# A hybrid diffusion backbone on one core: the low parts of U by VectorE, a transposed selection layout, and a gather whose last steps are spread

## The chip, the cores and the metric
One core of a Trainium2 chip runs the whole program in one launch. The metric is device time in microseconds (us) of that core; the median of several executions counts. Engines: PE is TensorE, DVE is VectorE, ACT is ScalarE, POOL is GpSimd, SP is SyncE, which issues most of the DMAs.

## The reference, cut to what matters
Two layers over 256 latent and 256 context tokens of width 1024. A layer is a token mixer followed by PEER, an expert retrieval, and the change touches PEER only (and in its second layer only the selection):

```python
q = (x @ wq).reshape(t, 8, 2, 64)
s = einsum('thpd,hpnd->thpn', q, keys)          # 2 x 128 scores per token and head
sv, si = lax.top_k(s, 16)
cand = sv[:, :, 0, :, None] + sv[:, :, 1, None, :]
best, pos = lax.top_k(cand, 16)                 # 8 heads x 16 experts per token
g = softmax(best)
act = gelu(einsum('tkd,td->tk', u_tab[eidx], x))
out = einsum('tk,tkd->td', g * act, v_tab[eidx])
```

There are 16384 experts of width 1024. The first layer handles all 512 tokens, the second one only the 256 latent tokens. Everything is float32.

## The kernel before
The kernel does not gather the experts of most tokens. It multiplies all of U with all tokens, weights the result with a mostly-zero gate matrix, and multiplies that with all of V. A float32 product is made of three matmuls over a high part `h` (rounded by ACT) and a low part `lo` (what rounding left, a subtraction on DVE or POOL); `halves` (L1221) makes both parts of a tile.

**Tiles of U and V.** U and V of a layer come in 128 tiles of 128x1024, 512 KB each. `u_mm` (L1235) is the product of tile j of U with the tokens: 24 matmuls into a PSUM tile `po`, of which there are two, po0 and po1, used in turn; ACT's Gelu empties it into `ga`. `split_u` (L1225) makes the parts `wh` and `wl` of U one tile ahead. Which engine makes `wl` is read from `lo_eng[0]`, and if that is None, POOL makes the odd tiles of the first layer and DVE the rest. During the routing `lo_eng[0]` is DVE in the first layer; at its end it is set to None, so POOL works in the sweep.

**The sweep** (the loop over j in the section that begins with `with ExitStack() as dx`): per tile of V, `gate` multiplies `ga` with the gate tile G and splits it into `Wh` and `Wl`, `split_v` makes `vh` and `vl` one tile ahead, and `v_mm` adds 18 matmuls of 512 columns per tile to six accumulators (three groups of 128 tokens in the first layer). Products of U run ahead of V by up to 20 tiles at the start and 10 from tile 64 on, so a tile of V and a product of U alternate on PE until tile 118, and after that V is alone.

**The gather.** In the first layer, the first 128 context tokens are not swept. `gather` (L1288) fetches their experts' rows with 256 indirect DMAs issued by POOL into three buffers `grow`, first 128 of U (a dot product on DVE, L1299), then 128 of V (a weighted sum on DVE into `gacc`, L1303). At its end it transposes `gacc` on PE in two halves into a `po` tile each (L386 is the transpose) and adds them to the stream `hT` (L1315). The sweep takes two steps of the generator per tile from tile 2, and a third on odd tiles from 25. Its 256 steps before the last part are used up at tile 109, where both halves of the last part are also made.

**The rows of the next layer's modulation** (`mod_rows`, 40 units in the first layer) start only when the generator of the gather is exhausted: two rows per tile from then on, the rest after the loop. Each row is a 512 KB load into the same `grow` buffers and two dot products on DVE for the first 16 rows (L512), one for the other 24 (L520). What DVE does in these steps is issued behind `vl` of the next tile (`issue_after(late.ins)`). After the loop, the sums of V are copied by ACT into `grow` buffers too (L1759), transposed, and added to `hT` (L1767); then the second layer begins.

**The selection** (`select`, L1400) runs once per group of 128 tokens, four times in the first layer and twice in the second, on DVE: 16 best of 60 candidates for each of 8 heads (`top16`), then arithmetic over 128 numbers per token on the positions. `best` and `pos` lie heads-outermost (8x16), `ab2` lies heads-innermost (16x8), so several instructions write with a stride. `scatter` builds the gate matrix from it. In the first layer the last selection, of the gathered tokens, comes after the last scatter; `fill` holds the early products of U, and one step of it is made per step of the routing.

**The order of the work.** The instructions of an engine are put in order by a planner at build time: what is ready sooner goes first, and among ready ones what the program emits first; a buffer is given to its next user when the last reader of the old content is done. On the chip every queue then runs in that order. So SP's loads, POOL's gathers and DVE's work each wait behind what stands ahead of them.

Of the kernel before, what the change touches and what calls it, by code (L numbers as in the profile page):

```python
# [8 lines left out]
F32 = mybir.dt.float32  # L9
F32R = mybir.dt.float32r  # L10
F16 = mybir.dt.float16
U32 = mybir.dt.uint32
I32 = mybir.dt.int32
AF = mybir.ActivationFunctionType
ALU = mybir.AluOpType
AX = mybir.AxisListType
# [3 lines left out]
P = 128  # L20
# [245 lines left out]
def body(ctx, tc, I, out, dbg=None):  # L266
# [21 lines left out]
    def po_tile():  # L288
        tick[0] ^= 1
        return psp.tile([P, 512], F32, name=f"po{tick[0]}")  # L290
# [62 lines left out]
    fill = Filler()  # L353
# [31 lines left out]
    def transpose(o, i):  # L385
        pe.transpose(o, i, ident)  # L386
# [183 lines left out]
    for l in range(DEPTH):  # L570
        last = l == DEPTH - 1
# [649 lines left out]
        def halves(h, lo, r, eng=dve):  # L1221
            act.activation(h, r, AF.Copy)  # L1222
            return eng.tensor_tensor(lo, r, h.bitcast(F32), op=ALU.subtract)  # L1223

        def split_u(j):  # L1225
            if j >= P:
                return
            h = wp.tile([P, D], F32R, name="wh", bufs=3)
            lo = wp.tile([P, D], F32R, name="wl", bufs=3)
            halves(h, lo, ur.pop(j), lo_eng[0] or (pool if not last and j % 2 else dve))  # L1230
            us[j] = (h, lo)

        def u_mm(j):
# [32 lines left out]
        def early(upto):  # L1266
            while nu[0] < upto:
                u_next()
                yield
# [12 lines left out]
        def gather():  # L1282

            rows = lambda: up.tile([P, D], F32, name="grow", bufs=3)
            gix, gw = gsel
            dot = up.tile([P, P], F32, name="gdot")
            for p, tab in ((0, I['UR']), (1, I['V'][l].rearrange("j i d -> (j i) d"))):
                q = []  # L1288
                for e in range(P + 2):
                    if e < P:  # L1290
                        q.append(rows())
                        pool.indirect_dma_start(out=q[-1], out_offset=None, in_=tab,  # L1292
                                                in_offset=bass.IndirectOffsetOnAxis(ap=gix[:, p, e:e + 1], axis=0))
                    if e < 2:
                        continue
                    e -= 2
                    g = q.pop(0)
                    if p == 0:
                        dve.scalar_tensor_tensor(g, g, 1.0, mtok, op0=ALU.mult, op1=ALU.mult, accum_out=dot[:, e:e + 1])  # L1299
                    elif e == 0:  # L1300
                        dve.tensor_scalar(acc, g, dot[:, e:e + 1], None, op0=ALU.mult)
                    else:
                        dve.scalar_tensor_tensor(acc, g, dot[:, e:e + 1], acc, op0=ALU.mult, op1=ALU.add)  # L1303
                    yield
                if p == 0:
                    act.activation(dot, dot, AF.Gelu)
                    dve.tensor_tensor(dot, dot, gw, op=ALU.mult)
            assert hT_back
            for h in range(2):
                ps = po_tile()  # L1310
                for k in range(4):
                    transpose(ps[:, k * 128:(k + 1) * 128], acc[:, (4 * h + k) * 128:(4 * h + k + 1) * 128])
                for k in range(4):
                    c = 4 * h + k
                    dve.scalar_tensor_tensor(hT[:, c, :128], ps[:, k * 128:(k + 1) * 128], mod[:, 40 + c, 0:1],  # L1315
                                             hT[:, c, :128], op0=ALU.mult, op1=ALU.add)
                yield
# [8 lines left out]
        with ExitStack() as tx:  # L1326
# [14 lines left out]
            KEYS = tk.tile([P, 1024], F32, name="keys")  # L1341
            pool.dma_start(KEYS, I['keys'][l])
            rep = sel.tile([P, 128], F32, name="rep", bufs=1)
            bits = sel.tile([P, 16], U32, name="bits", bufs=1)
            dve.memset(bits, 15)

            def top16(v, ix, x):
# [52 lines left out]
            def select(i):  # L1400

                sv, si = ranked.pop(i)

                lst = sel.tile([P, 2, 16, 8], F16, name="lst")
                act.activation(lst, si.rearrange("p (a h) r -> p a r h", a=2), AF.Copy)
                cand = sel.tile([P, 8, NC], F32, name="cand", bufs=1)
                for a, na, w, o in ROWS:
                    dve.tensor_tensor(cand[:, :, o:o + na * w].rearrange("p h (a b) -> p h a b", a=na),
                                      sv[:, 0:8, a:a + na][:, :, :, None].to_broadcast([P, 8, na, w]),
                                      sv[:, 8:16, :w][:, :, None, :].to_broadcast([P, 8, na, w]), op=ALU.add)  # L1410
                best = sel.tile([P, 8, 16], F32, name="best")
                pos = sel.tile([P, 8, 16], U32, name="pos")
                for h in range(8):
                    top16(best[:, h], pos[:, h], cand[:, h])
                    if h % 2:
                        yield


                ab2 = sel.tile([P, 2, 16, 8], F16, name="ab2")
                A, B = [ab2[:, z].rearrange("p k h -> p h k") for z in range(2)]  # L1420
                sl = sel.tile([P, 2, 8, 16], U32, name="sl", bufs=1)
                dve.tensor_scalar(sl[:, 0], pos, 3, None, op0=ALU.logical_shift_right)
                dve.tensor_scalar(sl[:, 1], pos, 2, None, op0=ALU.logical_shift_right)
                dve.tensor_scalar(A, sl[:, 0], -1.0, 0.0, op0=ALU.add, op1=ALU.max)
                dve.scalar_tensor_tensor(A, sl[:, 1], -5.0, A, op0=ALU.add, op1=ALU.max)
                dve.scalar_tensor_tensor(A, pos, -44.0, A, op0=ALU.add, op1=ALU.max)
                dve.tensor_scalar(sl[:, 0], pos, 16.0, None, op0=ALU.is_ge)
                for c in (32.0, 52.0, 52.0):
                    dve.scalar_tensor_tensor(sl[:, 0], pos, c, sl[:, 0], op0=ALU.is_ge, op1=ALU.add)
                dve.tensor_tensor(sl[:, 1], bits[:, None, :].to_broadcast([P, 8, 16]), sl[:, 0], op=ALU.logical_shift_right)  # L1430
                dve.tensor_tensor(sl[:, 1], pos, sl[:, 1], op=ALU.bitwise_and)
                dve.tensor_copy(B, sl[:, 1])
                ij = ijg[i] = sel.tile([P, 3, 16, 8], F32, name="ij")
                bm = sel.tile([P, 8], F32, name="bm")
                dve.tensor_copy(bm, best[:, :, 0])
                dve.tensor_tensor(best, best, bm[:, :, None].to_broadcast([P, 8, 16]), op=ALU.subtract)

                with tc.issue_after(evac[0].ins) if i < NG else nullcontext():
                    act.activation(best, best, AF.Exp)


                for z in range(2):
                    m = sel.tile([P, 16, 16, 8], F16, name="match", bufs=1)
                    dve.tensor_tensor(m, iotar[:, None].to_broadcast([P, 16, 16, 8]),
                                      ab2[:, z][:, :, None, :].to_broadcast([P, 16, 16, 8]), op=ALU.is_equal)
                    dve.tensor_tensor(m, m, lst[:, z][:, None].to_broadcast([P, 16, 16, 8]), op=ALU.mult)
                    for w in (8, 4, 2):
                        dve.tensor_tensor(m[:, :, :w], m[:, :, :w], m[:, :, w:2 * w], op=ALU.add)
                    dve.tensor_tensor(ij[:, z], m[:, :, 0], m[:, :, 1], op=ALU.add)
                    if z == 0:  # L1450
                        yield
                dve.tensor_reduce(bm, best, axis=AX.X, op=ALU.add)
                dve.reciprocal(bm, bm)
                dve.tensor_tensor(ij[:, 2].rearrange("p k h -> p h k"), best, bm[:, :, None].to_broadcast([P, 8, 16]), op=ALU.mult)
                if i < NG:

                    f = lambda x: x.rearrange("p k h -> p (k h)")
                    gix, gw = gsel
                    dve.scalar_tensor_tensor(gix[:, 0], f(ij[:, 0]), float(P), f(ij[:, 1]), op0=ALU.mult, op1=ALU.add)
                    dve.scalar_tensor_tensor(gix[:, 1], f(ij[:, 1]), float(P), f(ij[:, 0]), op0=ALU.mult, op1=ALU.add)  # L1460
                    dve.tensor_copy(gw, f(ij[:, 2]))
                yield
# [102 lines left out]
            def routing():  # L1565
# [31 lines left out]
                for z, _ in enumerate(end):  # L1597
                    next(others, 0)
                    if z == 8:
                        fill.add(early(ne))  # L1600
                    yield
                if NG:
                    yield from select(0)

# [1 line left out]
                for _ in range(per_step[0]):  # L1606
                    fill.step()
            fill.flush()
            lo_eng[0] = None


        with ExitStack() as dx:
# [205 lines left out]
```

## Time and profile before

| | |
|---|---|
| median of 3 runs | 3116.19 us (3100.6 to 3119.41) |
| the profiled execution | 3115.79 us, its span 3114.0 us |
| PE busy | 2956.3 us (95%) |
| DVE busy | 2339.7 us (75%) |
| ACT busy | 1448.6 us (47%) |
| POOL busy | 664.6 us (21%) |
| DMA | 661.43 MB, mean 212 GB/s |

The span begins with the first layer's mixer (to about 640 us), goes on with its scatter and selections (to 885), its sweep (885 to 1920), the second layer's mixer and routing (to about 2500) and its sweep. A row of busy times by stretch shows for each stretch how long every engine was busy; where PE is not busy all of it, the stretch has a limit other than PE. The granted clock of PE is 1.00 where it ran at 2.4 GHz throughout; a lower number mixes in time at 1.2 GHz. Matmuls of a row overlap: a matmul that lasts 389 ns is issued every 0.23 us.

### The profile page before, as it was taken

The page shows a single profiled execution, that of the slowest core. Times are in us where ns is not written, and L with a number is a line of the kernel's source. Part 1 is how long each engine was busy: PE and PEld are TensorE (multiplying, and loading weights), DVE is VectorE, ACT ScalarE, POOL GpSimd, SP SyncE. Part 2 cuts the span into 40 slices and gives each one's busy share as a digit, 9 for nine tenths or more (in the row PEclk, how much of TensorE's full clock was granted, in tenths as well). Part 3 has the DMA queues.
Part 4 walks back from the last instruction along what each step waited for, and adds up shares of the span by engine and source line. Part 5 has one row for each costly group of instructions (what it writes and reads, how often), then busy time and mean ns, then how long its engine had stood idle before and what let it go on. Part 6 is the DMA issues. An engine that isn't in the chain of part 4 may idle for free.

```text
span 3114.0 us, 47475 instructions
## 1 busy us (share of the span) xinstructions
PE 2956.3 (95%) x17500; PEld 2607.5 (84%) x17500; DVE 2339.7 (75%) x4764; ACT 1448.6 (47%) x2583; POOL 664.6 (21%) x428
## 2 busy tenths in 40 slices
PE   8999999988899999999999998999989999999998
PEld 5877777888788998888888886789988998889986
DVE  5775876799987877877877898868689767555555
ACT  5444422558843333323333234466458654554544
POOL 1001100310044455555555510100060000000000
PEclk9999999999999999999999998999999999999999
DMA  7232345534489888888888876344644689766644
GB/s 267 72 103 87 121 133 173 160 121 156 182 291 309 302 292 308 306 314 289 291 275 294 301 260 236 107 122 126 192 156 170 221 285 306 242 209 209 206 152 151
DMA packets 262504, 661.43 MB, mean 212 GB/s; under 512 B 21464, under 2 KB 113632, under 8 KB 261760
## 3 DMA queue, kind: packets, MB, share of 16 engines
q1 hardware_dynamic: 221808, 513.35, 50.3%
q0 software_dynamic: 40464, 145.05, 13.4%
q8 instruction: 137, 2.24, 0.3%
q14 instruction: 95, 0.78, 0.1%
HBM read 609.03 MB, written 49.29 MB: 211 GB/s over the span
## 4 chain that ended last, share of the span: by engine, by line
PE 49%; DVE 12%; DMA 11%; issue 9%; POOL 6%; ACT 2%; POOLq 0%; DVEq 0%; SPq 0%; ACTq 0%
PE mm L1664 7%; PE at L1664 7%; DMA grow<-in_V_dram,gix 6%; PE po L392 5%; PE po L390 5%; PE po L391 5%; PE mm L390 4%; PE mm L391 4%; PE mm L392 4%; POOL grow L1292 4%; PE at L1526 3%; DMA vr<-in_V_dram 2%; POOL wl L1223 2%; DMA grow<-in_UR_dram,gix 1%; DVE wl L1223 1%
## 5 line engine op out<-in xcount | busy, mean ns | idle before, releaser
L392 PE MATMUL po<-nh,wl 128*128 128x384 f32 (+1 forms) x2048 | 642.4, 314 | 33.8 <-DVE wl L1223 30.4
L390 PE MATMUL po<-nh,wh 128*128 128x384 f32 (+1 forms) x2048 | 642.6, 314 | 13.0 <-DVE hT L1315 5.4
L1222 ACT ACTIVATE vh<-vr 128x1024 fp32r<-128x1024 f32 x254 | 269.5, 1061 | 613.7 <-DMA vr<-in_V_dram 530.5
L392 PEld LDWEIGHTS po<-nh,wl 128*128 128x128 f32 x2048 | 392.7, 192 | 44.2 <-DVE wl L1223 39.0
L390 PEld LDWEIGHTS po<-nh,wh 128*128 128x128 f32 x2048 | 393.7, 192 | 23.7 <-DVE hT L1315 6.1
L1223 DVE TENSOR_TENSOR vl<-vr,vh 128x1024 fp32r<-128x1024 f32 x254 | 334.4, 1317 | 99.6 <-ACT vh L1222 99.3
L1222 ACT ACTIVATE wh<-wraw 128x1024 fp32r<-128x1024 f32 x256 | 269.7, 1054 | 238.7 <-PE po L391 188.8
L390 PE MATMUL mm<-nh,wh 128*128 128x256 f32 (+1 forms) x1056 | 347.6, 331 | 10.8 <-ACT nh L487 3.9
L391 PE MATMUL po<-nl,wh 128*128 128x384 f32 x1024 | 348.0, 340 | 0.0
L392 PE MATMUL mm<-nh,wl 128*128 128x256 f32 (+1 forms) x1056 | 342.2, 325 | 0.4 <-POOL wl L328 0.4
L391 PE MATMUL mm<-nl,wh 128*128 128x256 f32 (+1 forms) x992 | 323.6, 327 | 0.0
L1223 DVE TENSOR_TENSOR wl<-wraw,wh 128x1024 fp32r<-128x1024 f32 x187 | 232.1, 1244 | 104.8 <-ACT wh L1222 104.7
L327 ACT ACTIVATE wh<-wraw 128x1024 fp32r<-128x1024 f32 x156 | 164.7, 1058 | 298.5 <-PE mm L391 189.6
L391 PE MATMUL po<-nh,wh 128*128 128x256 f32 x1024 | 290.5, 284 | 0.0
L1664 PE MATMUL mm<-vl,Wh 128*128 128x512 f32 x635 | 251.8, 397 | 11.6 <-DVE vl L1223 11.3
L1664 PE MATMUL mm<-vh,Wh 128*128 128x512 f32 x635 | 249.1, 392 | 1.9 <-ACT vh L1222 1.9
L1664 PE MATMUL at<-vh,Wh 128*128 128x512 f32 x635 | 248.9, 392 | 0.0
L1664 PE MATMUL mm<-vh,Wl 128*128 128x512 f32 x635 | 248.2, 391 | 0.0
L1664 PE MATMUL at<-vl,Wh 128*128 128x512 f32 x635 | 248.0, 391 | 0.0
L1664 PE MATMUL at<-vh,Wl 128*128 128x512 f32 x635 | 248.0, 391 | 0.0
L1223 POOL TENSOR_TENSOR wl<-wraw,wh 128x1024 fp32r<-128x1024 f32 x69 | 173.1, 2512 | 306.6 <-DVE best L1349 218.2
L1299 DVE SCALAR_TENSOR_TENSOR grow<-grow,mtok 128x1024 f32<-128x1024 f32 x128 | 167.7, 1327 | 91.1 <-DMA grow<-in_UR_dram,gix 91.0
(367 smaller groups left out, 6501.8 us busy)
## 6 DMA issues: line engine op xcount, KB each, us to landing
wraw<-in_U_dram SPq DMA_DIRECT2D x256, 512.0 KB, 4.3
vr<-in_V_dram SPq DMA_DIRECT2D x254, 512.0 KB, 4.6
wraw<-in_W_dram SPq DMA_DIRECT2D x190, 512.0 KB, 3.7
gd<-gblk SPq DMA_DIRECT2D x80, 512.0 KB, 4.7
G<-gd SPq DMA_DIRECT2D x32, 768.0 KB, 8.2
grow<-in_W_dram SPq DMA_DIRECT2D x48, 512.0 KB, 5.0
G<-gd SPq DMA_DIRECT2D x32, 512.0 KB, 5.7
mw<-in_W_dram SPq DMA_DIRECT2D x16, 512.0 KB, 9.0
```

The lines of the kernel that those rows point to most:

```text
L327: act.activation(h, r, AF.Copy)
L390: pe.matmul(ps, w[0], x[0], start=first, stop=False)
L391: pe.matmul(ps, w[0], x[1], start=False, stop=False)
L392: pe.matmul(ps, w[1], x[0], start=False, stop=last)
L1222: act.activation(h, r, AF.Copy)
L1223: return eng.tensor_tensor(lo, r, h.bitcast(F32), op=ALU.subtract)
L1292: pool.indirect_dma_start(out=q[-1], out_offset=None, in_=tab, in_offset=bass.IndirectOffsetOnAxis(ap=gix[:, p, e:e + 1], axis=0))
L1299: dve.scalar_tensor_tensor(g, g, 1.0, mtok, op0=ALU.mult, op1=ALU.mult, accum_out=dot[:, e:e + 1])
L1526: pe.matmul(ps4[:, :, z], A[:, :, z], C[:, z, :, h], start=h == 1, stop=h == 0)
L1664: pe.matmul(accs[i][h], w[a][:, i * 128:(i + 1) * 128], v[b][:, h * 512:(h + 1) * 512], start=j == 0 and a + b == 0, stop=j == P - 1 and a ...
```

## The change
Four edits. (1) In the first layer's sweep `lo_eng[0]` stays DVE, so the odd tiles' `wl` go from POOL to DVE; the second layer is unchanged in this. (2) `best`, `pos` and their arithmetic lie heads-innermost: `top16` now writes with a stride of 8 elements and the 128-element instructions are contiguous. (3) At the end of the gather, each of the two halves has four empty steps ahead of its transposes and three between them and the additions, 16 steps in place of 2. (4) In the first layer the last two early products of U are emitted after the last scatter instead of from its ninth step on.

```diff
@@ split_u
-            halves(h, lo, ur.pop(j), lo_eng[0] or (pool if not last and j % 2 else dve))
+            halves(h, lo, ur.pop(j), lo_eng[0])
@@ gather
             for h in range(2):
+                for _ in range(4):
+                    yield
                 ps = po_tile()
                 for k in range(4):
                     transpose(ps[:, k * 128:(k + 1) * 128], acc[:, (4 * h + k) * 128:(4 * h + k + 1) * 128])
+                for _ in range(3):
+                    yield
                 for k in range(4):
...
@@ select
-            bits = sel.tile([P, 16], U32, name="bits", bufs=1)
+            bits = sel.tile([P, 8], U32, name="bits", bufs=1)
...
-                best = sel.tile([P, 8, 16], F32, name="best")
-                pos = sel.tile([P, 8, 16], U32, name="pos")
+                best = sel.tile([P, 16, 8], F32, name="best")
+                pos = sel.tile([P, 16, 8], U32, name="pos")
                 for h in range(8):
-                    top16(best[:, h], pos[:, h], cand[:, h])
+                    top16(best[:, :, h], pos[:, :, h], cand[:, h])
...
-                A, B = [ab2[:, z].rearrange("p k h -> p h k") for z in range(2)]
-                sl = sel.tile([P, 2, 8, 16], U32, name="sl", bufs=1)
+                A, B = ab2[:, 0], ab2[:, 1]
+                sl = sel.tile([P, 2, 16, 8], U32, name="sl", bufs=1)
...
-                dve.tensor_reduce(bm, best, axis=AX.X, op=ALU.add)
+                dve.tensor_reduce(bm, best.rearrange("p k h -> p h k"), axis=AX.X, op=ALU.add)
...
@@ routing
                     if z == 8:
-                        fill.add(early(ne))
+                        fill.add(early(ne - 2 if NG else ne))
                     yield
+                fill.add(early(ne))
                 if NG:
                     yield from select(0)
...
             fill.flush()
-            lo_eng[0] = None
```

## Rows read from the trace of the kernel before

**Rows 1.** The page: busy time, share of the span and instructions of each engine.
```profile
PE 2956.3 (95%) x17500; PEld 2607.5 (84%) x17500; DVE 2339.7 (75%) x4764; ACT 1448.6 (47%) x2583; POOL 664.6 (21%) x428
```

**Rows 2.** Busy time by stretch: from:to, length, each engine, PE clock, DMA share, GB/s.
```profile
640.00:885.00 245.00, 208.90 (x1432) 194.20 (x1431) 230.45 (x839) 178.95 (x436) 7.59 (x3) 0.95 0.45 162
885.00:1200.00 315.00, 312.37 (x1541) 281.25 (x1542) 243.05 (x328) 109.75 (x152) 161.85 (x104) 0.99 0.90 306
1200.00:1750.00 550.00, 523.42 (x2588) 470.50 (x2587) 434.13 (x422) 175.82 (x251) 297.14 (x190) 0.99 0.86 296
1750.00:1810.00 60.00, 49.06 (x234) 43.61 (x233) 50.70 (x58) 16.91 (x24) 21.50 (x13) 0.89 0.82 281
1810.00:1872.00 62.00, 62.00 (x319) 57.10 (x319) 61.96 (x106) 19.83 (x28) 9.46 (x3) 1.00 0.82 271
```

**Rows 3.** Groups of PE, 1200 to 1750 us: count, busy, mean ns, idle before and its releasers.
```profile
L392 PE MATMUL po<-nh,wl 128*128 128x384 f32 x483 | 166.4, 345 | 19.9 <-DVE wl L1223 17.6 <-POOL wl L1223 2.1
...
L1664 PE MATMUL mm<-vl,Wh 128*128 128x512 f32 x190 | 74.6, 393 | 6.1 <-DVE vl L1223 6.1
```

**Rows 4.** Groups of POOL, 880 to 1800 us.
```profile
L1292 POOL DMA_INDIRECT grow<-in_V_dram,gix x128 | 183.7, 1435 | 206.1 <-DVE gacc L1303 159.5 <-DMA grow<-in_V_dram,gix 24.8 <-issue 9.7
...
L1223 POOL TENSOR_TENSOR wl<-wraw,wh 128x1024 fp32r<-128x1024 f32 x49 | 119.1, 2431 | 15.6 <-ACT wh L1222 14.7
```

**Rows 5.** Groups of DVE, 885 to 1785 us.
```profile
L1303 DVE SCALAR_TENSOR_TENSOR gacc<-grow,gdot,gacc 128x1024 f32<-128x1024 f32 x127 | 167.1, 1316 | 87.3 <-DMA grow<-in_V_dram,gix 85.7
L1223 DVE TENSOR_TENSOR vl<-vr,vh 128x1024 fp32r<-128x1024 f32 x109 | 157.0, 1440 | 1.1 <-ACT vh L1222 1.1
L1223 DVE TENSOR_TENSOR Wl<-ga,Wh 128x384 fp32r<-128x384 f32 x92 | 113.2, 1232 | 0.8 <-ACT Wh L1222 0.8
L1223 DVE TENSOR_TENSOR wl<-wraw,wh 128x1024 fp32r<-128x1024 f32 x48 | 58.5, 1218 | 0.0
L1653 DVE TENSOR_TENSOR ga<-ga,G 128x384 f32<-128x384 f32 x95 | 53.9, 574 | 4.0 <-DMA G<-gd 4.0
```

**Rows 6.** Timeline of DVE near 1750 us: start, duration, instruction, idle before it.
```profile
1749.87 3.28 DVE L1223 TENSOR_TENSOR Wl<-ga,Wh 128x384 fp32r<-128x384 f32 x1
...
1758.62 1.29 DVE L1303 SCALAR_TENSOR_TENSOR gacc<-grow,gdot,gacc 128x1024 f32<-128x1024 f32 x1 [1.82 <-DMA grow<-in_V_dram,gix]
```

**Rows 7.** Timeline of POOL in the same stretch.
```profile
1750.32 2.40 POOL L1223 TENSOR_TENSOR wl<-wraw,wh 128x1024 fp32r<-128x1024 f32 x1
1752.88 1.09 POOL L1292 DMA_INDIRECT grow<-in_V_dram,gix  x1 [0.16 <-issue]
1755.74 1.86 POOL L1292 DMA_INDIRECT grow<-in_V_dram,gix  x1 [1.78 <-DVE gacc L1303]
1757.91 0.94 POOL L1292 DMA_INDIRECT grow<-in_V_dram,gix  x1 [0.30 <-issue]
```

**Rows 8.** Timeline of PE at the end of the gather.
```profile
1792.44 1.12 PE L386 MATMUL po<-kc,gacc 128*128 128x128 f32 x4 [4.13 <-ACT ga L1249]
...
1801.08 0.69 PE L390 MATMUL po<-nh,wh 128*128 128x384 f32 x1 [5.38 <-DVE hT L1315]
```

**Rows 9.** Timeline of DVE where the modulation rows begin.
```profile
1785.09 1.22 DVE L1223 TENSOR_TENSOR vl<-vr,vh 128x1024 fp32r<-128x1024 f32 x1
1786.22 1.22 DVE L512 SCALAR_TENSOR_TENSOR junk<-grow,mtok 128x1024 f32<-128x1024 f32 x1
```

**Rows 10.** Instructions on the grow buffers: ns min/median/max, first and last start.
```profile
L520 DVE SCALAR_TENSOR_TENSOR grow<-grow,gacc x24: 1211/1218/1226, 1860.4 to 1916.1; 128x1024 f32<-128x1024 f32 x24
```

**Rows 11.** Waits of ACT, 1895 to 1925 us: total, times, longest.
```profile
ACT grow L1759 <- DVE grow L520: 7.4, 1, 7.4
```

**Rows 12.** Groups of DVE, 640 to 900 us: two instructions of the selection.
```profile
L1429 DVE SCALAR_TENSOR_TENSOR sl<-pos,sl 128x128 uint32<-128x128 uint32 x12 | 4.3, 360 | 0.0
...
L1425 DVE SCALAR_TENSOR_TENSOR ab<-sl,ab 128x128 f16<-128x128 uint32 x4 | 3.0, 748 | 0.0
```

**Rows 13.** Waits of PE, 860 to 900 us.
```profile
PE mm L1664 <- ACT Wh L1222: 6.0, 1, 6.0
```

More of the change, by code (lines that the diff above doesn't have):

```diff
@@ L1429, in select @@
                     dve.scalar_tensor_tensor(sl[:, 0], pos, c, sl[:, 0], op0=ALU.is_ge, op1=ALU.add)
-                dve.tensor_tensor(sl[:, 1], bits[:, None, :].to_broadcast([P, 8, 16]), sl[:, 0], op=ALU.logical_shift_right)
+                dve.tensor_tensor(sl[:, 1], bits[:, None, :].to_broadcast([P, 16, 8]), sl[:, 0], op=ALU.logical_shift_right)
                 dve.tensor_tensor(sl[:, 1], pos, sl[:, 1], op=ALU.bitwise_and)
@@ L1434, in select @@
                 bm = sel.tile([P, 8], F32, name="bm")
-                dve.tensor_copy(bm, best[:, :, 0])
-                dve.tensor_tensor(best, best, bm[:, :, None].to_broadcast([P, 8, 16]), op=ALU.subtract)
+                dve.tensor_copy(bm, best[:, 0])
+                dve.tensor_tensor(best, best, bm[:, None, :].to_broadcast([P, 16, 8]), op=ALU.subtract)
                 with tc.issue_after(evac[0].ins) if i < NG else nullcontext():
@@ L1451, in select @@
                         yield
-                dve.tensor_reduce(bm, best, axis=AX.X, op=ALU.add)
+                dve.tensor_reduce(bm, best.rearrange("p k h -> p h k"), axis=AX.X, op=ALU.add)
                 dve.reciprocal(bm, bm)
-                dve.tensor_tensor(ij[:, 2].rearrange("p k h -> p h k"), best, bm[:, :, None].to_broadcast([P, 8, 16]), op=ALU.mult)
+                dve.tensor_tensor(ij[:, 2], best, bm[:, None, :].to_broadcast([P, 16, 8]), op=ALU.mult)
                 if i < NG:
```

## The prediction
> **What bounds the kernel now.** I read the page's busy times first: PE is busy for 95% of the span [rows 1], so a gain can only come from the 5% where it idles and from time at the lower clock. The busy times by stretch say where that is [rows 2]. In 640 to 885 us (scatter and selections) DVE is busy for 230.45 of 245 us and PE waits for it. In 885 to 1200 us PE is full. In 1200 to 1750 us it idles 550 − 523.42 = 26.6 us, and a granted clock of 0.99 costs about 0.01 × 550 = 5.5 us more: 32 us, the first sum that the change can touch. In 1750 to 1810 us it idles 10.9 us at a clock of 0.89 (another 6.6 us): 17.5 us, the second. In 1810 to 1872 us it is full again, 319 matmuls in 62 us, so a tile with a product (18 + 24 = 42 matmuls) takes 42 × 62 / 319 = 8.2 us, and the 18 of V alone 4.1 us by their issue step of 0.23 us. The groups of PE name the releasers in the middle stretch: `wl` made by DVE 17.6 us, by POOL 2.1 us, `vl` 6.1 us [rows 3].
>
> **Edit 1, the low parts of U.** 49 of POOL's subtractions stood in 880 to 1800 us, 2.431 us each; on DVE one takes 1.218 us, so DVE gets 49 × 1.218 = 60 us of work and POOL loses 119 us [rows 4, 5]. But the trace shows that they were not free for DVE. A `Wl` lasted 3.28 us while POOL's subtraction ran from 1750.32 to 1752.72 us, where the mean of its like (`ga` times G, same shape) is 0.574 us [rows 5 to 7]. Over the sweep, `Wl` lost 92 × (1232 − 574) ns = 60.5 us and `vl` 109 × (1440 − 1218) ns = 24.2 us [rows 5]: 85 us, more than the 60 us that come in. DVE is therefore about 25 us freer over the sweep, not fuller, and it never was full (434 of 550 us).
>
> The second half of this edit is POOL's queue. The gather behind the subtraction could be issued only at 1752.88 us; its row landed late, and DVE's sum waited 1.82 us for it, with the next `wl` behind [rows 6, 7]. Such waits sum to 85.7 us [rows 5], and they are what makes DVE's `wl` late for PE. Without the subtraction that gather goes out about 2.4 us earlier. Against this: a gather's issue took 0.94 us where DVE stood idle and 1.86 us beside DVE's work [rows 6, 7], so 49 more DVE instructions can stretch some issues by 0.92 us, at most 45 us in all, on a queue that waits 206 us for buffers anyway [rows 4].
>
> The Trainium skill has a rule for this that speaks against the edit: "SBUF — State Buffer", section "SBUF: two separate sides", says that POOL cannot write the descriptors of its DMAs while a certain kind of DVE instruction holds the port pair that the two share, and that the loser of that pair waits for the whole instruction. The rows agree with the waiting, in both directions; by the first half alone edit 1 would cost something, by both it gains.
>
> How much of the 32 us comes back? All of it if PE is full again; bounded below by 5 us, if DMA latencies take the place of the waits. PE was full at 306 GB/s in 885 to 1200 us, and the middle stretch would need 296 × 550 / 518 = 314 GB/s [rows 2], just above that. I take two thirds, **−22 us** (ends −5 and −32).
>
> **Edit 3, the end of the gather.** Now both halves are transposed in one tile: the second waits 4.13 us for a Gelu to empty its `po`, and the next product waits 5.38 us for the additions [rows 8]. Spread over tiles, these 9.5 us and most of the clock loss around them (17.5 us less 9.5 leaves 8) should go; a held `po` tile can still make one product wait for the additions, up to the 5.4 us of before. Alone this would give 13 us.
>
> But the generator's steps pay for it. 14 steps more at 2.5 per tile put its end at tile 115 in place of 109, and the modulation rows begin only then. They are bound to that tile on DVE: the first stood directly behind `vl` of tile 110, at 1786.22 us [rows 9], and the last of the L520 dots began at 1916.1 us [rows 10]. They already set the end of the sweep: ACT's copy of the sums waited 7.4 us for a `grow` buffer that such a row held [rows 11]. So what is late is late at the layer's boundary. The start moves to 1786.2 + 6 × 8.2 = 1835.4 us (this counts the stall as gone). From there DVE has 16 rows of two dots (16 × 2 × 1.22 = 39 us), 24 of one dot with its small instructions (24 × 1.3 = 31 us), the gate and `vl` of 11 tiles (11 × 2.2 = 24 us) and two `wl` (2.4 us): 96 us, ending at 1931 us. If the last 16 rows, with V's loads done, keep the spacing that the 24 had ((1916.1 − 1860.4) / 23 = 2.42 us in place of 1.3), it is 18 us more, 1949 us. In before the last dot ended at 1917.3 us. Edit 3 as a whole thus costs 14 to 32 us; PE has only 10 × 4.1 + 2 × 8.2 = 57 us of work left to put beside DVE's 96. I take **+18 us**, near the lower end, because the slow spacing of the 24 rows came while V was loading too. SP's queue also counts: six rows' loads fewer stand ahead of V's loads in tiles 109 to 114, and as many more stand among them after 115; that is inside the ends.
>
> **Edit 2, the selection.** An instruction with a strided f16 write took 0.748 us where a like one without took 0.360 us [rows 12]; with four such per selection the layout can save some 4 × 0.39 = 1.5 us. `top16` now writes eight numbers with a stride, which no row shows: bounded below by nothing, above by the same excess per number ((748 − 360) / 128 = 3 ns, so 8 × 3 = 24 ns) over some 50 instructions, 1.2 us. Six selections, all while DVE is nearly full: −9 to +7 us, net −0.3 us each, **−2 us**.
>
> **Edit 4, the two products kept back.** They are to cover PE's 6.0 us of waiting before the first tile of V [rows 13]. They cost DVE nothing new, since their `wl` only move, behind the last scatter. At least −6 us and a little clock; at worst they delay the selection by two `wl` (+2.4 us). The end of the selection is DVE's, so I take **−3 us**.
>
> **Sum.** −22 + 18 − 2 − 3 = −9 us on the profiled execution's 3115.79 us (span 3114.0), which lies 0.4 us below the median shown: **3107 us**. Own range: 3115.8 − 32 + 14 − 9 − 6 = 3083 to 3115.8 − 5 + 32 + 5 = 3148.
>
> **Rivals.** (a) *The rows of the modulation stay hidden.* If rows emitted after the loop, which are not bound to a tile, are put earlier, or the additions no longer wait for the buffers, edit 3 gives its 13 us alone: 3115.8 − 22 − 13 − 5 = 3076. For it: loads were seen to be issued well ahead. Against: rows 9 and 11. Chance 0.13.
> (b) *DVE's queue becomes the wait in the sweep* (slower). In the middle stretch the tiles whose `wl` DVE made cost PE 17.6 us, POOL's 2.1 us, at about equal numbers [rows 3]. If all tiles fare like DVE's, that is 15.5 us more instead of 22 less: 3107 + 37.5 = 3145, and 3150 with little from edits 2 and 4. It decides if the sum's waits for gathered rows stay at 85.7 us though POOL is free. Chance 0.13.
> (c) *The middle stretch keeps its pace*, because SP issues the load of V behind that of U, which waits for a `wl`: edit 1 gives 3 us, 3107 + 19 = 3126. Chance 0.14.
> The forecast keeps 0.60.
>
> **How the numbers follow.** About 1% (31 us) is what a measurement can tell from no change here. Below 3085 lie most of (a) and a little of the forecast's range, 0.11 + 0.09 = 0.20. Above 3147 lies half of (b) and the forecast's upper end beside (c), 0.07 + 0.05 = 0.12. Between: 0.68. The range takes in (c), (b)'s first number and most of (a): 3076 to 3146.
>
> **What would show it.** Right: no POOL subtraction in the sweep; means of `Wl` and `vl` near 0.57 and 1.22 us; PE idling under 12 us in 550 us of the middle; no wait for L1315 at the gather's end; the first L512 about six tiles before the end of U's products (near tile 116's `vl`), and an idle PE of 10 to 35 us behind the last tile of V. Wrong: waits of PE for `wl` above 20 us in the middle (b), or additions of the residual that start with the end of V, as before (a).

## The result and the profile after

The changed kernel takes 3071.6 us (median of 4 runs, 3066.16 to 3072.57) against 3111.22 us (the kernel before has four runs here, one more than ahead of the prediction): a ratio of 0.9871, 95% interval 0.9835 to 0.9907. The forecast was 3107 us with a range of 3076 to 3146, so the direction was right, but the time lies outside the range, 4 us below its lower end.

Busy times of the changed kernel by stretch, cut at the places that answer to [rows 2] (from:to, length, then each engine, PE clock, DMA share, GB/s; the last row is the end of the first layer's sweep):

```profile
640.00:874.00 234.00, 203.15 (x1392) 189.20 (x1391) 217.15 (x807) 176.41 (x432) 0.00 (x0) 0.96 0.43 162
874.00:1189.00 315.00, 314.94 (x1575) 284.12 (x1575) 250.93 (x373) 118.71 (x162) 127.31 (x96) 1.00 0.93 329
1189.00:1700.00 511.00, 511.00 (x2596) 466.14 (x2595) 398.31 (x446) 183.12 (x249) 214.00 (x159) 1.00 0.90 320
1700.00:1760.00 60.00, 60.00 (x308) 54.66 (x307) 30.49 (x38) 21.61 (x30) 2.44 (x2) 1.00 0.61 202
1760.00:1822.00 62.00, 62.00 (x305) 54.90 (x304) 57.07 (x104) 20.21 (x29) 0.00 (x0) 1.00 0.69 220
1822.00:1878.00 56.00, 23.64 (x98) 17.93 (x97) 44.05 (x96) 8.61 (x16) 2.73 (x5) 0.70 0.76 254
```

PE is full from 874 to 1822 us at a clock of 1.00. The middle stretch takes 511 us for 2596 matmuls, where it took 550 us for 2588. Then PE is busy for 23.64 of 56 us, at a clock of 0.70. The waits of PE there (1700 to 1880 us), and of ACT (1800 to 1900 us):

```profile
PE at L386 <- ACT grow L1764: 31.8, 2, 30.2
PE mm L1669 <- DVE vl L1223: 0.3, 1, 0.3
```

```profile
ACT grow L1764 <- DVE grow L520: 35.4, 1, 35.4
```

This is the wait of [rows 11], 7.4 us before: the copy of the sums waits for a `grow` buffer that the modulation rows hold. Those rows begin directly behind the second half's additions (L1320), which stand behind `vl` of tile 116 (compare [rows 9]); the timeline of DVE:

```profile
1763.02 1.23 DVE L1223 TENSOR_TENSOR vl<-vr,vh 128x1024 fp32r<-128x1024 f32 x1 [0.44 <-ACT vh L1222]
1764.16 1.12 DVE L1320 SCALAR_TENSOR_TENSOR hT<-po,mod,hT 128x128 f32<-128x128 f32 x4
1765.19 1.22 DVE L512 SCALAR_TENSOR_TENSOR junk<-grow,mtok 128x1024 f32<-128x1024 f32 x1
```

The instructions on `grow` (ns min/median/max, first and last start, to set beside [rows 10]):

```profile
L520 DVE SCALAR_TENSOR_TENSOR grow<-grow,gacc x24: 1212/1224/1226, 1824.9 to 1873.6; 128x1024 f32<-128x1024 f32 x24
```

The groups of DVE in the sweep, 874 to 1710 us, which answer to [rows 5]:

```profile
L1303 DVE SCALAR_TENSOR_TENSOR gacc<-grow,gdot,gacc 128x1024 f32<-128x1024 f32 x127 | 162.9, 1283 | 82.3 <-DMA grow<-in_V_dram,gix 81.3
...
L1223 DVE TENSOR_TENSOR vl<-vr,vh 128x1024 fp32r<-128x1024 f32 x109 | 133.0, 1220 | 6.8 <-ACT vh L1222 6.8
L1223 DVE TENSOR_TENSOR wl<-wraw,wh 128x1024 fp32r<-128x1024 f32 x97 | 118.4, 1220 | 0.7 <-ACT wh L1222 0.7
L1658 DVE TENSOR_TENSOR ga<-ga,G 128x384 f32<-128x384 f32 x94 | 51.5, 552 | 2.4 <-DMA G<-gd 2.4
L1223 DVE TENSOR_TENSOR Wl<-ga,Wh 128x384 fp32r<-128x384 f32 x91 | 50.3, 553 | 7.1 <-ACT Wh L1222 6.9
```

`Wl` fell from a mean of 1232 to 553 ns and `vl` from 1440 to 1220, while 49 more `wl` came in: DVE had more instructions to run and was busy for less time in all. The wait for gathered rows of V hardly moved, 85.7 to 81.3 us.

To place the whole difference I took from PE's timeline when it began tile 0, tile 109 and tile 127 of V (runs of 18 matmuls), and the start of the first addition of the residual. All columns are in us; two marks side by side are the time from one to the other:

| profiled execution | tile 0 | 0 to 109 | 109 to 127 | 127 to residual | residual to end | span |
|---|---|---|---|---|---|---|
| before | 885.1 | 898.5 | 126.5 | 7.1 | 1196.8 | 3114.0 |
| after | 874.2 | 850.0 | 113.1 | 37.4 | 1195.6 | 3070.3 |
| difference | −10.9 | −48.5 | −13.4 | +30.3 | −1.2 | −43.7 |

### The profile page after: what moved, and what is told of

It is laid out like the page before. It is cut to its first block, busy times and chain, and to the rows that moved or that the text cites. A ratio compares the mean times of both kernels' runs of the same rounds, so it can differ in the third digit from the quotient of the medians.

```text
span 3070.3 us, 47403 instructions
## 1 busy us (share of the span) xinstructions
PE 2933.1 (96%) x17500; PEld 2595.1 (85%) x17500; DVE 2280.2 (74%) x4818; ACT 1460.4 (48%) x2583; POOL 512.9 (17%) x374
## 4 chain that ended last, share of the span: by engine, by line
PE 69%; DVE 11%; DMA 4%; issue 2%; ACT 2%; POOL 0%; DVEq 0%; ACTq 0%; SPq 0%; POOLq 0%
PE mm L1669 12%; PE at L1669 12%; PE po L392 9%; PE po L390 9%; PE po L391 9%; PE mm L390 4%; PE mm L391 4%; PE mm L392 4%; PE at L1531 3%; DMA vr<-in_V_dram 2%; DMA wraw<-in_W_dram 1%; DMA grow<-in_W_dram 1%; DVE wl L1223 1%; DVE rep L1356 1%; DVE ohB L1493 1%
## 5 line engine op out<-in xcount | busy, mean ns | idle before, releaser
L392 PEld LDWEIGHTS po<-nh,wl 128*128 128x128 f32 x2048 | 391.4, 191 | 14.2 <-DVE wl L1223 13.7
L1223 DVE TENSOR_TENSOR vl<-vr,vh 128x1024 fp32r<-128x1024 f32 x254 | 310.5, 1222 | 107.4 <-ACT vh L1222 107.2
L1223 DVE TENSOR_TENSOR wl<-wraw,wh 128x1024 fp32r<-128x1024 f32 x241 | 293.8, 1221 | 124.1 <-ACT wh L1222 124.0
L1292 POOL DMA_INDIRECT grow<-in_UR_dram,gix x128 | 169.4, 1324 | 482.6 <-DVE gix L1465 241.4
L390 PEld LDWEIGHTS mm<-nh,wh 128*128 128x128 f32 x1056 | 203.1, 193 | 39.1 <-issue 5.6
```

The costliest lines, as they stand in the source:

```text
L390: pe.matmul(ps, w[0], x[0], start=first, stop=False)
L392: pe.matmul(ps, w[1], x[0], start=False, stop=last)
```

## The experiments

Theory A: edit 1 takes 48 us of waits out of the sweep, edit 3 costs about 17 us. The rivals are that the new order which edits 2 to 4 bring sped the sweep, and that edit 3 was a gain.

**Each edit alone, and edit 3 undone.** The diffs are the parts shown ahead: `e1_only` has the `split_u` line and no reset of `lo_eng`, `e3_only` the two empty loops in `gather`, `e24` the selection and the early products; `no3` is the changed kernel without the empty loops, so edits 1, 2 and 4:

```diff
             for h in range(2):
-                for _ in range(4):
-                    yield
                 ps = po_tile()
...
-                for _ in range(3):
-                    yield
```

> Edit 1 alone on the kernel before. Theory A (edit 1 takes the waits of the sweep away, 48 us between the first tile of V and tile 109; edit 3 costs 17 us): 3111 - 48 = 3063 us, tiles 0 to 109 of V in about 850 us instead of 898.5, PE still waiting some 10 us at the end of the gather and no idle PE behind the last tile of V. Rival B (edit 1 gives the 22 us that were forecast, and the rest of the gain comes from the new order that edits 2 to 4 bring): 3089 us, tiles 0 to 109 in about 876 us.

> Edit 3 alone. Theory A: the stall of 13 us goes, and 30 us of idle PE come behind the last tile of V: 3111 + 17 = 3128 us. Rival B (spreading the steps is a gain): 3111 - 13 = 3098 us, with no idle PE behind the last tile.

> Edits 2 and 4 without 1 and 3. Theory A: the first tile of V starts some 6 us earlier than in the kernel before and the sweep is unchanged: 3105 us. Rival B: their new order speeds the sweep too: 3090 us or less. Rival C: they do nothing: 3111 us, and the earlier start of the sweep came from POOL's two subtractions before it, which edit 1 moves.

> The changed kernel with edit 3 undone (edits 1, 2 and 4). Theory A: rows of the modulation start at tile 109 again and end with V, so the idle PE of 30 us behind the last tile goes and a stall of up to 13 us at the end of the gather comes back: 3072 - 17 = 3055 us. Rival B (edit 3 was needed): 3072 + 13 = 3085 us.

| kernel | median us | ratio to before (95%) | tile 0 | 0 to 109 | 109 to 127 | 127 to residual |
|---|---|---|---|---|---|---|
| e1_only | 3061.68 | 0.9839 (0.9806 to 0.9873) | 880.8 | 861.1 | 123.6 | 6.2 |
| e3_only | 3130.27 | 1.0074 (1.0046 to 1.0102) | 879.0 | 895.8 | 113.5 | 37.3 |
| e24 | 3099.45 | 0.9961 (0.9939 to 0.9984) | 869.9 | 888.7 | 127.8 | 6.4 |
| no3 | 3047.99 | 0.9813 (0.9784 to 0.9842) | 874.9 | 849.9 | 117.4 | 5.1 |

Edit 1 alone gains 48.7 us, more than the whole change (39.6). In tiles 0 to 109 it gives 37.4 of the 48.5 us, between the two expectations; the other 11 us came only with edits 2 and 4 beside it, so the rival has a share in the sweep. Edit 3 alone is 0.7% slower: it takes 13 us from tiles 109 to 127 and puts 30 us behind them. The waits of PE in `e3_only`, 1740 to 1930 us, name the same buffer:

```profile
PE at L386 <- ACT grow L1763: 31.5, 2, 30.6
```

Without edit 3 the changed kernel is 23.6 us faster than with it. The stall at the end of the gather hardly returned (117.4 us, with rows of the modulation among the tiles, against 113.1); why is not shown, since with edit 1 alone these tiles took 123.6 us. In `no3` tiles 0 to 109 take 849.9 us without edit 3, so that edit has no share in the sweep.

**Edits 2 and 4 apart.** `e2_only` has the new layout of the selection alone, `e4_only` the two products kept back alone.

> Edit 2 alone. By the durations of the run with the new layout a selection of 128 tokens is about 1.3 us shorter on DVE, so 6 selections give at most 8 us, and 3 to 8 us if DVE bounds them: 3103 to 3108 us. Rival (edit 4 is what gains): 3111 us.

> Edit 4 alone. Edits 2 and 4 together gained 11 us, the first tile of V starting 10 to 15 us earlier. If keeping two products back does it, 3100 to 3104 us and the wait before the first tile of V (6.0 us) is gone; if it is the selection's layout, 3108 to 3111 us.

3099.74 us (ratio 0.9954, 0.9941 to 0.9967) and 3106.52 us (0.9967, 0.9952 to 0.9982). By these ratios each gains 10 to 14 us alone, and together they gain no more (11 us). Edit 2 gained more than the 8 us expected at most, and `e4_only` came out between its two expectations. Edit 4 shortens the wait of [rows 13], 6.0 us, but does not end it; in `e4_only` and then in `e2_only`, 850 to 900 us:

```profile
PE mm L1665 <- ACT Wh L1222: 2.5, 1, 2.5
```

```profile
PE mm L1664 <- ACT Wh L1222: 5.1, 1, 5.1
```

3.5 us of the 10 are seen in that wait. Edit 2's part is in the durations of the selection ([rows 12] were 748 and 360 ns); the changed kernel, 640 to 900 us:

```profile
L1434 DVE SCALAR_TENSOR_TENSOR sl<-pos,sl 128x128 uint32<-128x128 uint32 x12 | 3.4, 286 | 0.0
...
L1457 DVE TENSOR_REDUCE bm<-best 128x8 f32<-128x128 f32 x4 | 1.6, 390 | 0.0
L1430 DVE SCALAR_TENSOR_TENSOR ab<-sl,ab 128x128 f16<-128x128 uint32 x4 | 1.1, 282 | 0.0
```

An instruction that reads and writes f16 with a stride went from 748 to 282 ns, one that only writes so from 458 to 219; the reduction, now strided, rose from 266 to 390; the strided results of `top16` cost about 7 ns an instruction (`MAX8` 209 to 216, `FIND_INDEX8` 215 to 221). Summed over a selection of the first layer, from `e4_only` (old layout) to `e2_only`, the arithmetic is 2.0 us shorter and `top16` 0.4 us longer: some 1.55 us a selection, 9 us in six. The rest of both gains may lie in the order that the planner finds, which any edit shifts; that stays open.

**What in POOL's subtraction cost the sweep.** My working gave two ways: DVE stalls beside it, and the gathers wait behind it on POOL's queue. A third is that it holds U's raw buffer for 2.4 us, and SP's next loads with it. All five kernels are `no3` with POOL work added in the sweep, on odd tiles of U up to 115; DVE still makes every low part. The diff is cut to POOL's instruction: that of `pool_sub`, and in place of its last line those of `pool_set`, `pool_other` (`pool_twice` does it twice) and `pool_hold`:

```diff
             halves(h, lo, r, lo_eng[0])
+            if extra and j % 2 and j < 116:
+                pool.tensor_tensor(extra[0], r, h.bitcast(F32), op=ALU.subtract)     # pool_sub
+                    pool.memset(extra[0], 0.0)   # pool_set: twice, behind a gather
+                    pool.tensor_tensor(extra[0], extra[0], extra[0], op=ALU.subtract)   # pool_other: behind a gather
+                    pool.memset(r, 0.0)          # pool_hold: twice
```

> Edits 1, 2 and 4 (3048 us), and POOL repeats the subtraction of the odd tiles of U up to 115 into a spare buffer that nobody reads; DVE still makes every low part. If POOL's instruction itself was the cost (it blocks DVE on the way to the memory, holds back the gathers behind it, and holds U's raw buffer longer), the 40 to 48 us come back though DVE's and PE's own work is that of the fast kernel: tiles 0 to 109 in 885 to 905 us, 3085 to 3105 us, means of Wl over 1.0 us. Rival (what helped was only that DVE delivers a low part in 1.2 us where POOL took 2.4): little changes, 3048 to 3055 us.

> As pool_sub, but POOL fills the spare buffer with zeros twice in place of the subtraction, behind a gather: its queue is held for about as long, and it reads nothing. If the gathers held back on POOL's queue were the cost, most of the 40 to 48 us come back (3080 us or more, means of Wl near 0.55 us). If it was DVE's stall beside a POOL instruction that reads two buffers, and the fill does not stall DVE, the time stays at 3048 to 3055 us. Should the fill stall DVE too, the means of Wl and vl show it, and the run tells nothing of the queue alone.

> Edits 1, 2 and 4, and POOL subtracts the spare buffer from itself on odd tiles of U up to 115, behind a gather: a two-input POOL instruction of the same length that reads nothing of U and holds no buffer of U. If DVE's stall beside a POOL instruction with two inputs is the cost, most of the loss of the run with the repeated subtraction comes back: tiles 0 to 109 in 880 to 905 us instead of 850, 3080 to 3115 us, means of ga, Wl and vl well above 0.55, 0.55 and 1.22 us. Rival (U's raw buffer, released only after POOL's 2.5 us, and the loads of U and V queued behind that on SP): 3048 to 3058 us, tiles 0 to 109 in about 850 us though the means may rise.

> As the run in which POOL subtracts the spare buffer from itself (tiles 0 to 109 in 866 us, DVE's instructions 62 us longer in sum), with two such subtractions in place of one. If DVE's stalls alone set what is lost, DVE loses 100 us or more as in the run that repeats U's subtraction, and tiles 0 to 109 take 885 to 910 us (3080 to 3105 us). Rival (the rest was U's raw buffer held by POOL): 866 to 880 us, 3060 to 3075 us.

> Edits 1, 2 and 4, and POOL writes zeros twice into the raw buffer of each odd tile of U up to 115 after DVE has made the low part, so that the buffer is given back some 2 us later; POOL reads nothing. If the late release (SP issues U's next load and the load of V queued behind it later) is what the stalls leave unexplained, tiles 0 to 109 take 870 to 890 us instead of 850 with DVE's means unchanged, 3065 to 3090 us. Rival (the release has slack): 850 to 855 us, 3048 to 3055 us.

Groups of POOL and DVE, 870 to 1710 or 1720 us, in `pool_set`:

```profile
L1235 POOL MEMSET junk<- 128x1024 f32 x94 | 91.4, 972 | 0.1
```

```profile
L1661 DVE TENSOR_TENSOR ga<-ga,G 128x384 f32<-128x384 f32 x93 | 51.0, 553 | 2.3 <-DMA G<-gd 2.3
L1223 DVE TENSOR_TENSOR Wl<-ga,Wh 128x384 fp32r<-128x384 f32 x90 | 49.7, 552 | 0.6 <-ACT Wh L1222 0.6
```

in `pool_twice`:

```profile
L1235 POOL TENSOR_TENSOR junk<-junk 128x1024 f32<-128x1024 f32 x88 | 169.1, 1922 | 1.7
```

```profile
L1223 DVE TENSOR_TENSOR vl<-vr,vh 128x1024 fp32r<-128x1024 f32 x98 | 134.6, 1374 | 0.0
...
L1223 DVE TENSOR_TENSOR Wl<-ga,Wh 128x384 fp32r<-128x384 f32 x80 | 103.8, 1298 | 0.1
L1662 DVE TENSOR_TENSOR ga<-ga,G 128x384 f32<-128x384 f32 x84 | 53.0, 635 | 3.0 <-DMA G<-gd 3.0
```

and of DVE in `pool_sub`:

```profile
L1659 DVE TENSOR_TENSOR ga<-ga,G 128x384 f32<-128x384 f32 x85 | 93.2, 1100 | 1.7 <-DMA G<-gd 1.7
L1223 DVE TENSOR_TENSOR Wl<-ga,Wh 128x384 fp32r<-128x384 f32 x82 | 71.2, 869 | 0.0
```

From such groups, taken from tile 0 to tile 109 of each kernel, I summed what DVE's instructions took above their means in `no3` (dots 1221, weighted sums 1282, `vl` 1218, `ga` and `Wl` 551 ns):

| kernel | median us | POOL adds | DVE's excess, us | 0 to 109, us | above no3 |
|---|---|---|---|---|---|
| no3 | 3047.99 | nothing | 0 | 849.9 | 0 |
| pool_hold | 3039.43 | 91 us, fills of U's buffer | 1 | 850.1 | 0 |
| pool_set | 3051.28 | 91 us, fills | 1 | 850.5 | 1 |
| pool_other | 3059.44 | 92 us, subtraction | 62 | 866.5 | 17 |
| pool_sub | 3119.83 | 115 us, subtraction of U | 106 | 910.2 | 60 |
| pool_twice | 3137.07 | 181 us, two subtractions | 140 | 931.2 | 81 |

The two kernels whose POOL work reads nothing lose nothing, though POOL's queue is held for as long as in `pool_other`, and though in `pool_hold` SP's loads of U did wait for the fills (880 to 1700 us):

```profile
SPq L1219 <- POOL wraw L1234: 325.6, 47, 11.7
```

Those whose POOL instruction reads lengthen DVE's instructions, and PE waits for the low parts that DVE makes. In `pool_sub`, 877 to 1786 us (before, from tile 0 to tile 109, it was 8.4 us for `vl` and 19.0 for `wl` of DVE; in `pool_set` and `pool_hold` PE waits for nothing there):

```profile
PE mm L1670 <- DVE vl L1223: 20.2, 10, 5.0
PE po L392 <- DVE wl L1223: 19.1, 17, 2.8
```

So neither the queue nor the buffer alone is the cause; DVE's time is left. More excess goes with a longer sweep, but the excess is no price: 62 us of it cost 17, and 106 cost 60. All three kernels missed the times expected of them, `pool_other` below (880 to 905 us expected for tiles 0 to 109), `pool_sub` and `pool_twice` above. The kernel before does not fit the series either. Its excess was 111 us (`Wl` and `vl` alone 87, by [rows 5]), and it saved DVE the 60 us of low parts that POOL made: 51 us more of DVE's time than after, for a sweep that was 48.5 us longer, where `pool_other` lost 17 us with more. Which instruction is hit, and when, must count. In the kernel before, the odd low parts themselves also came later (2.43 us on POOL against 1.22 on DVE); these five kernels, in which DVE makes every low part, do not test what that cost. And `pool_other` is clearer in its profile than in its median, which is 11 us above `no3`, little more than near-alike kernels differ by.

The Trainium skill, "SBUF — State Buffer", section "SBUF: two separate sides", says that a DVE instruction with two inputs in SBUF competes for the shared ports only with a POOL instruction that reads SBUF, and that the loser waits for the whole of it. The runs agree: 552 ns beside fills, up to 1298 ns in the mean beside subtractions.

**Rows of the modulation earlier.** The third step of the gather on odd tiles from tile 2, with edit 3 (`early_gath`) and without (`no3_early`):

```diff
-                        for _ in range((2 if j > 1 else 0) + (j > 24 and j % 2)):
+                        for _ in range((2 if j > 1 else 0) + (j > 1 and j % 2)):
```

> The changed kernel (3071.6 us, with edit 3), the third step of the gather on odd tiles from tile 2 on in place of 25: the gather ends some 4 to 5 tiles earlier, so the rows of the modulation begin near tile 111. If the late start of the rows is the 30 us of idle PE behind V, it shrinks to 0 to 5 us and the time is 3044 to 3052 us. Rival (the spread steps themselves cost): 3070 us. Third: the faster gather makes DMA the limit in the first 40 tiles, PE waits there, and the gain is lost: 3060 us or more with tiles 0 to 40 in over 300 us instead of 293.

> Edits 1, 2 and 4 with the same earlier third step: a try at a version faster than all. In the run with edits 1, 2 and 4 the last nine tiles took 42.2 us instead of 38.2, DVE being busy with rows; starting them five tiles earlier can win these 4 us: 3042 to 3048 us. If DMA limits the first 40 tiles, slower: 3050 to 3060 us.

3079.87 us (0.9902, 0.987 to 0.9934) and 3065.36 us (0.9843, 0.98 to 0.9885): both slower than without. The time of `early_gath` is that of its third expectation (tiles 0 to 40 took 305 us), and `no3_early` lies above both of its own. The rows did begin earlier, at 1757.3 us behind `vl` of tile 112 in place of 116, and the long wait shrank from 31.8 us to 6.6 us, `early_gath` from 1345 us on:

```profile
PE at L386 <- ACT grow L1763: 6.6, 2, 4.6
```

So the late start of the rows is what edit 3 costs. But the first 60 tiles took 469.4 us instead of 445.6. `early_gath` in its first 469 us of the sweep, then the changed kernel in its first 446 us:

```profile
876.00:1345.00 469.00, 453.74 (x2231) 404.84 (x2232) 359.05 (x520) 156.77 (x223) 195.51 (x147) 0.99 0.92 322
```

```profile
874.00:1320.00 446.00, 445.94 (x2235) 403.02 (x2235) 349.13 (x511) 165.01 (x225) 181.42 (x137) 1.00 0.93 329
```

The same matmuls, and DMA no busier than in the faster run (322 against 329 GB/s), while PE waited, mostly for `vl` (8.6 us). More gathered rows per tile may have held it up: DVE waited 108 us for gathered rows in that stretch, 80 in the changed kernel, and never for `vh`, though ACT waited 237 us for V's loads, against 46. Whether DMA or DVE's order made `vl` late was not separated.

**The rest of POOL's subtractions.** `no_pool` is `no3` with the other 54 subtractions of POOL on DVE as well:

```diff
-                (pool if order[m][1] == 'wq' or ... else dve).tensor_tensor(lo, r, h.bitcast(F32), op=ALU.subtract)
+                dve.tensor_tensor(lo, r, h.bitcast(F32), op=ALU.subtract)
...
-        lo_eng = [pool if last else dve]
+        lo_eng = [dve]
```

> Edits 1, 2 and 4, and every other subtraction of POOL (54, in the mixers, the query weights and the second layer's early products) on DVE too: a try at a faster version. If each of them stalls DVE by about 2 us where DVE is nearly full, it gains 10 to 30 us: 3020 to 3040 us. Rival: in those stretches PE has 47 of 50 us of work and DVE is not what it waits for, so nothing or a small loss, 3045 to 3060 us.

3035.56 us (0.974, 0.9726 to 0.9754), the lowest median here, and within the 3020 to 3040 us expected of a gain. Its first tile of V starts at 863.5 us against 874.9 in `no3`, tiles 0 to 109 are as long (850.4 us), and behind the first layer's sweep it takes 5 us more: the gain lies ahead of the sweep, where the busy times of before showed DVE nearly full. It is 12 us below `no3` but 4 us below `pool_hold`, which kept these 54 subtractions, so a gain of this size is not clear of the scatter between near-alike kernels.

## Why the prediction was wrong

In medians, step by step, edit 1 brought −48.7 us (`e1_only`), edits 2 and 4 beside it −13.7 (`no3`) and edit 3 beside all three +23.6; the prediction had −22, −5 and +18.

- **The step that failed is the size of edit 1: the 32 us that the middle stretch was said to hold, and the two thirds taken of them.** Forecast −22 us between −5 and −32. `e1_only` showed −48.7 us in the median; its tiles 0 to 109 were 37.4 us shorter, and 48.5 us with the other edits beside it. First, the 32 us were too few. In the middle stretch PE's waits were 26.6 us, and I put 5.5 us for the clock. The pace says more: 2596 matmuls took 511.0 us after, so the 2588 of [rows 2] needed 509.4 us, and 523.4 us were busy. 14 us were hidden in busy time, 41 in all. Counting tiles would have shown it: by the prediction's own figure a tile with a product takes 8.2 us, and tiles 60 to 109 took 8.9 each. Second, I took two thirds although no row spoke for a remainder. Tiles 10 to 109 took 826.3 us before, 789.1 in `e1_only` and 783.7 after: edit 1 alone gave back nearly all that was lost there.
- **A full stretch that was not full.** [Rows 2] show 2.6 us of waiting and a clock of 0.99 from 885 to 1200 us, which I read as full: the first ten tiles took 72.2 us and now take 66.3. This was not edit 1's doing, for in `e1_only` they took 72.0; it came with the edits together.
- **Which half of edit 1 it was.** I split it into DVE's stalls and POOL's queue, and gave the queue the waits of the sum for gathered rows (85.7 us) as what makes `wl` late. They stayed at 81.3 us while PE's waits went. The dots' waits for U's rows fell from 91.0 to 73.2 us, but were 90.8 in `pool_set`, which lost nothing. A queue held by fills cost nothing. The runs bear out the half that I called "not free for DVE": its excess of 111 us is 0 in `e1_only`. How its size makes the loss stays open.
- **The rule that spoke against edit 1.** The prediction priced 49 more DVE instructions at up to 45 us on POOL's queue. The mean issue of a gather of V's rows fell, 1435 ([rows 4]) to 1362 ns: no such cost is seen. The sentence of the Trainium skill given with the fills above, on instructions with two inputs, is the one that bears on these subtractions, and it speaks for the edit.
- **Edit 3: right.** Forecast +18 us, with the 13 us of the stall counted as gone; measured −13.4 + 30.3 = +16.9 us in the profile, and 23.6 us by the run without it. The rows lasted 1765.2 to 1874.8 us, 110 us, within the 96 to 114 worked out, and the copies waited behind them.
- **Edits 2 and 4: −5 us forecast, −12 us** by the table (11 by their run), and what they add in the sweep beside edit 1. The layout saves 1.55 us a selection instead of 0.3: more instructions became shorter than the four that were counted (2.0 us against 1.5), and strided results of `top16` cost 7 ns and not 24. In the own range of the sum, the upper end counts 5 us for these two edits, where their own ends (+7 and +2.4) make 9; the result lies at the other end.
- **The rivals.** (b) set as its condition that the waits for gathered rows stay near 85.7 us. They did, and PE was full: those waits did not reach PE, so the condition did not decide it. (a) was out: rows kept their tile. (c) was out: no wait of PE is left in the sweep.

## What to carry to other kernels

A subtraction that POOL takes over is not free if DVE is busy beside it: price it by how far DVE's instructions in the same stretch exceed the same shapes elsewhere, and set that sum against what the instruction would take on DVE. The sum says which way to go; what the stretch loses by it was here anything from a quarter to more than half, so try it. Measure what a stretch can give back by its pace (tiles or matmuls per us against a stretch that runs full), not by PE's idle time alone. A step that is spread out delays whatever is emitted when it is exhausted: find who waits for that, and whether it already sets the end of the stage.

## What the runs showed of the hardware that was not expected

A POOL fill of 128x1024 took 964 to 972 ns and did not lengthen DVE's two-input instructions (552 ns), while a subtraction of the same shape took 1922 to 2502 ns and raised single groups of them to means of 811 to 1298 ns; which group it hits depends on where it falls, so the cost is not a fixed amount per POOL instruction. Near-alike kernels differ by some 9 us in the median (3039 and 3048 us for `pool_hold` and `no3`), with tile 0 at 869 and 875 us: differences of that size between edits say little here.
